# Order of TensorE in the first pairs of both MLP heads, and the place of the splits of squares

## The chip, the cores and the metric

The kernel runs on one core of a Trainium2 chip. The metric is the device time of one execution in microseconds (us); lower is better. The core has five engines with a queue each: TensorE (PE in the profile, its weight loads PEld) multiplies, VectorE (DVE), ScalarE (ACT) and GpSimd (POOL) work on elements, SyncE (SP) starts most transfers. An engine takes its own queue in order and waits on semaphores for the others.

## The reference

Two sequences of 512 tokens with 1024 features pass through a trunk of two layers. Cut to what matters:

```python
def sq_relu_mlp(h, w_up, w_down):
    a = jnp.maximum(h @ w_up, 0)
    return (a * a) @ w_down

def trunk(x, ...):
    for i in range(2):
        if i == 0:
            x = x + fourier_mix(rms_norm(x, fourier_norm), fourier_w_out)
        else:
            x = x + gqa_attention(rms_norm(x, attn_norm), ...)   # ends with o @ w_o
        x = x + sq_relu_mlp(rms_norm(x, mlp_norm[i]), w_up[i], w_down[i])
    return rms_norm(x, final_norm)
```

`rms_norm` divides a token's features by the root of their mean square and multiplies by a gain. Each MLP needs this norm over all 1024 features before its first product, and the output needs it once more.

## The kernel before, in words

Features lie on the partitions, tokens along the free dimension: `xt(q, fo)` is feature block `fo` (of 8) of sequence `q`, 128x512 in float32. Each float32 operand is split into a high half (a cast on ScalarE, line 86) and a low half (a subtraction on VectorE, line 87), and a product takes three matmuls per slice (`mm3`, lines 81 to 83, and `product`, line 962).

**The norm of transposed features.** `square` (line 167) squares a feature block on ScalarE; GpSimd adds the squares into `acc[q]` (line 171). With `alone=True` the last square is not added but kept in `apart[q]`. `Rows.split_all` splits `acc[q]` and, if there is one, `apart[q]` into halves. `Rows.root` multiplies them by a column of -1 on TensorE (line 206), which sums over the features; three activations follow on ScalarE (lines 207 to 209), and `Rows.rows` ends the row of inverse roots with two instructions on VectorE (lines 212 and 214). `Blocks.gain` (line 239) multiplies a feature block by its gain on ScalarE, `Blocks.norm` (line 254) by the row of inverse roots on VectorE.

**The MLP's two products** go by a Strassen-like scheme over blocks of both sequences. `Blocks.first` makes the operands `b11` (index 0 and 1) and `b21` (2 and 3) of sequence 0: norm, high half on ScalarE; `first_lo` makes the low half on VectorE (line 271). `second_sums` makes, for both sequences, norms, sums and differences (lines 311 to 323) and their halves, as a generator that the loop over pairs drives.

**The head of `first_product`.** Blocks of `w_up` come in pairs. Of the first `AHEAD` = 8 pairs, the loop computes the products with sequence 0 alone, while sequence 1's norm is being made: `Pair.first` multiplies by `b11` into a PSUM bank and copies it (ScalarE, line 995); `Pair.second` goes on in the same bank with `b21`, then come ReLU and square (lines 976 and 977). `split_row` splits a pair's weights (lines 86 and 87). Within the loop: `split_sums(1)` at p = 2, `root(1)` at p = 3, `spread(1)` (which is `Rows.rows`) at p = 4; second of pair 0 comes after second of pair 1. After the loop `rest` computes the remaining five products of each pair.

**W_o** ends attention and stands ahead of the second head. Blocks `m` = 0 to 3 are multiplied by operands `b11` and `b21`, then `t2`, `t3`, `t4`, and last `t1` and `b22` in the order of `turn()` (eight products, j = 0 to 7). In the t4 loop the add of line 1766 ends sequence 0's odd features, `square` and `gain` follow; after the loop comes `split_sums(0)`; in the last loop `root(0)` stands at j = 1 and `spread(0)` at j = 2, `first` and `first_lo` from j = 2 on.

**The tail** computes the last four blocks of the second MLP's down product. `project(0, fo)` and `project(1, fo)` run over eight feature blocks of sequence 0 and of half of sequence 1; between them `tokens(2)` and `tokens(3)` transpose two tiles of tokens, which `tile` computes with tokens on the partitions. `oa` and `ob` hold the output of the transposed part; `write` (line 1889) multiplies by the row of inverse roots and sends the output away.

**Who sets the order.** The Tile framework orders the instructions of each engine by its own plan from the dependencies. Within `tc.manual_schedule(engines={...})` the engines named take their instructions in the order written: all five in the tail, TensorE in the W_o part and in the second products, VectorE in part of `rest`. The head loop of `first_product` has no such block. `behind(x, y)` puts one instruction behind another in an engine's order without a semaphore.

Of the kernel before, what the change touches and what calls it, by code (L numbers as in the profile page):

```python
# [13 lines left out]
F32R = mybir.dt.float32r  # L14
BF16 = mybir.dt.bfloat16
AF = mybir.ActivationFunctionType
# [3 lines left out]
P = 128  # L20
# [24 lines left out]
def trunk_kernel(ctx, tc, x_in, xt_in, y_out, tables, rope, gfour, gcol, grow, gfin,  # L45
                 w_four, w_nyq, w_qkv, w_o, w_a22, w_up, w_row2, w_row4, w_sum2, w_sum4, w_down):
    nc = tc.nc
# [17 lines left out]
    def slot(shape, dt):  # L65
        return act.tile(shape, dt, tag="u4", name=nm("u"))
# [10 lines left out]
    def f32(ap):  # L77
        return ap.bitcast(F32)
# [6 lines left out]
    def split(dst_hi, dst_lo, src, eng=nc.vector):  # L85
        hi = nc.scalar.copy(dst_hi, src)  # L86
        return hi, eng.tensor_sub(dst_lo, src, f32(dst_hi))  # L87
# [64 lines left out]
    xs, acc, apart = {}, {}, {}  # L152
# [6 lines left out]
    def xt(q, fo):  # L159
        return xs[q, fo // 2][:, fo % 2]  # L160
# [23 lines left out]
    class Rows:  # L184
# [2 lines left out]
        def __init__(self, q, n=512):  # L187
            self.q, self.n, self.parts = q, n, []

        def split(self, x):  # L190
            h = slot([P, 2, self.n], F32R)
            made = split(h[:, 0], h[:, 1], x[:, : self.n])
            self.parts += [h[:, 0], h[:, 1]]
            return made

        def split_all(self):
            for x in [acc[self.q]] + ([apart.pop(self.q)] if self.q in apart else []):
                made = self.split(x)
            return made

        def root(self):
            n, o = self.n, ps()
# [25 lines left out]
    class Blocks:  # L228
# [7 lines left out]
        def gain(self, q, fo):  # L236
            if (q, fo // 2) not in self.f:
                self.f[q, fo // 2] = slot([P, 2, 512], F32)
            nc.scalar.activation(self.f[q, fo // 2][:, fo % 2], xt(q, fo), AF.Copy,
                                 scale=gc[:, self.g0 + fo : self.g0 + fo + 1])  # L240

        def split_sums(self, q):
            self.r[q] = Rows(q)
            return self.r[q].split_all()

        def root(self, q):
            self.r[q].root()
# [705 lines left out]
              for op in ROW + SUM} for l in range(2)]  # L953
    plain = [drm.tile([P, 2, 512], F32, name=f"plain_{f}") for f in range(2 * PLAIN)]

    def product(o, w, h, first=True):

        n = len(h)
        for k in range(n):
            sl = slice(k * P, (k + 1) * P)  # L960
            for i, (x, y) in enumerate(((0, 0), (0, 1), (1, 0))):
                nc.tensor.matmul(o, w[x][:, sl], h[k][y], start=first and k + i == 0,  # L962
                                 stop=k == n - 1 and i == 2, skip_group_check=not first)

    wo_added = []

    def first_product(l, blocks, rows, ahead):
# [120 lines left out]
        todo = blocks.second_sums()  # L1088
        pairs = [Pair(p) for p in range(NP)]
        for p in range(AHEAD):  # L1090
            if p == 4:
                blocks.spread(1)
            pair = pairs[p]
            if p < len(rows):
                pair.row = rows[p]
            else:
                pair.load()
                pair.split_row()
                if p == 3 and wo_added:
                    behind(pair.low, wo_added[0])  # L1100
            pair.first()
            if p == 2:
                blocks.split_sums(1)
            if p == 3:
                blocks.root(1)
            if p > 0:
                pair.second()
            if p == 1:
                pairs[0].second()
            if p > 3:  # L1110
                for _ in range(3):
# [653 lines left out]
    def add(x, o):  # L1765
        return nc.vector.tensor_add(x, o, x)
# [9 lines left out]
    with tc.manual_schedule(engines={ET.PE}):  # L1776
        o = {}
        for m, i in turn():
            if i == 0:
                o[m] = ps()  # L1780
            product(o[m], ahead[m][i], heads_out.operand(("b11", "b21")[i]), i == 0)
            if i:
                add(xs[0, m][:, 0], o[m])
                list(load_kept())
            else:
                nc.scalar.copy(e[m], o[m])
            if m + i > 1:
                next(todo)
        load_xs(1, park[1])
        o = {}  # L1790
        for k, name in enumerate(("t2", "t3", "t4")):
            h = heads_out.operand(name)
            for m in range(4):
                if k < 2:
                    o[m] = ps()
                product(o[m], ahead[4 + 2 * k + m // 2][m % 2], h, k < 2)
                if k == 0:
                    add(e[m], o[m])
                    square(0, 2 * m)
                    add(xs[0, m][:, 1], e[m])  # L1800
                elif k == 1:
                    add(xs[1, m][:, 1], o[m])
                    add(xs[1, m], e[m].unsqueeze(1).broadcast_to([P, 2, 512]))
                    blocks.gain(0, 2 * m)
                else:
                    add(xs[0, m][:, 1], o[m])
                    square(0, 2 * m + 1, alone=m == 3)
                    blocks.gain(0, 2 * m + 1)
                    put_away(0, m)
                if m % 2:  # L1810
                    list(load_kept())
                next(todo, None)
                if k == 2 and m < 2:
                    rows.append(halves(load_raw(w_up[1, 2 * m]), home=lent))
        o, lows = {}, []
        blocks.split_sums(0)
        for j, (m, i) in enumerate(turn()):
            if i == 0:
                o[m] = ps()
            product(o[m], ahead[10 + m][i], heads_out.operand(("t1", "b22")[i]), i == 0)  # L1820
            fo = 2 * m + 1 - i
            added = add(xt(1, fo), o[m])
            if 3 < j < 6:
                behind(lows[j - 4], added)
            square(1, fo, first=1)
            blocks.gain(1, fo)
            if i:
                put_away(1, m)
            if j == 1:
                blocks.root(0)  # L1830
            if j == 2:
                blocks.spread(0)
            if 1 < j < 6:
                normed = blocks.first(j - 2)
                if j == 5:
# [66 lines left out]
    with tc.manual_schedule(engines={ET.PE, ET.Activation, ET.DVE, ET.Pool, ET.SP}):  # L1902
        oa, ob, oc, oe = OutT(0, 4), OutT(1, 2), Out(2), Out(3)
        for fo in range(KC):
            project(0, fo, ws, [a[0] for a in ats])
            square(0, fo)
            oa.gain(fo)
        xtok = [tokens(2), tokens(3)]
        for fo in range(KC):
            project(1, fo, ws, [a[1] for a in ats], 256)  # L1910
            square(1, fo, 256, fo == KC - 1)
            ob.gain(fo)
            if fo == 1:
                oa.r.split_all()
            if fo == 2:
                oa.r.root()
            if fo == 3:
                oa.spread()
            if fo > 3:
                oa.write(fo - 4)  # L1920

        x, z = xtok
# [20 lines left out]
        def write(y, r, sl):  # L1943
            nc.scalar.activation(y[:, sl], y[:, sl], AF.Copy, scale=r)

        ob.r.split_all()
        o = [tile(2, 0, 512, 3, ob.r.root)]
        add(x, o[0], 0, 512)
        gain(x, y[0], 0)
# [191 lines left out]
```

## Time and profile before

| | |
|---|---|
| Median of three runs | 1674.67 us (1674.65 to 1674.84) |
| The profiled execution | 1674.12 us |
| Its span, first to last instruction | 1672.3 us |
| TensorE busy | 1656.0 us (99%) |
| VectorE busy | 1264.4 us (76%) |
| ScalarE busy | 884.9 us (53%) |
| GpSimd busy | 395.7 us (24%) |
| TensorE clock granted | 0.999 of full |

A row of the timeline has the start in us from the span's start, the length in us, engine and line, operation, output and inputs by the program's names, the count of instructions merged, and in brackets the idle time of the engine before it with what ended it. `PE ps L962` is a matmul of `product` into a PSUM bank. A page's row that groups instructions has their busy time and mean duration in ns. A row of windows has the stretch, its length, and for TensorE, its weight loads, VectorE, ScalarE and GpSimd the busy time with the count; then the granted clock, the share of the DMA engines and GB/s.

### The profile page before, as it was taken

How to read it: one execution, taken by the hardware profiler on the slowest of the kernel's cores; microseconds unless marked ns; L12 is line 12 of the kernel's file. 1: busy time of each engine (PE TensorE's matmuls, PEld its weight loads, DVE VectorE, ACT ScalarE, POOL GpSimd, SP SyncE). 2: the span in 40 equal slices, each digit the busy share in tenths (PEclk: the TensorE clock that was granted, in tenths of full speed). 3: DMA queues.
4: the chain of work that ended last, by engine and by line, in shares of the span. 5: the costliest groups of instructions: out<-in, count | busy, mean ns of one | idle time of the engine just before them, and what ended most of it. 6: DMA issues, size and time to landing. Idle time of an engine off the chain costs nothing.

```text
span 1672.3 us, 22127 instructions
## 1 busy us (share of the span) xinstructions
PE 1656.0 (99%) x7768; PEld 1379.8 (83%) x7768; DVE 1264.4 (76%) x1818; ACT 884.9 (53%) x1572; POOL 395.7 (24%) x365
## 2 busy tenths in 40 slices
PE   9999999999999999999999999999999999999997
PEld 8987888888888888888888888788888888888886
DVE  8889776557786879868788877777854487978865
ACT  7776444446343425448688855554544552433335
POOL 3331444221000001226444303004422220000002
PEclk9999999999999999999999999999999999999999
DMA  9843554459775757525401156335544696657522
GB/s 308 254 158 114 207 196 176 145 177 370 245 232 166 253 172 231 176 66 196 164 1 38 64 187 221 108 120 178 200 153 163 230 375 191 223 160 245 167 101 102
DMA packets 122193, 302.48 MB, mean 181 GB/s; under 512 B 12345, under 2 KB 13497, under 8 KB 122081
## 3 DMA queue, kind: packets, MB, share of 16 engines
q1 hardware_dynamic: 98720, 253.53, 43.4%
q0 software_dynamic: 8960, 21.05, 5.9%
q10 hardware_dynamic: 14400, 26.48, 4.2%
q8 instruction: 61, 1.00, 0.2%
q14 instruction: 52, 0.42, 0.1%
HBM read 217.59 MB, written 82.38 MB: 179 GB/s over the span
## 4 chain that ended last, share of the span: by engine, by line
PE 91%; DVE 6%; ACT 1%; issue 1%; DMA 0%; POOL 0%; DVEq 0%; SPq 0%; ACTq 0%; POOLq 0%
PE ps L962 71%; PE ps L83 6%; PE ps L81 6%; PE ps L82 6%; PE ps L1558 2%; DVE u L254 1%; DVE u L87 1%; DVE u L1889 0%; DVE u L271 0%; PE ps L1537 0%; DVE w L87 0%; ACT w L86 0%; DMA u<-x 0%; DVE t L214 0%; DVE u L312 0%
## 5 line engine op out<-in xcount | busy, mean ns | idle before, releaser
L962 PE MATMUL ps<-u,w 128*128 128x512 f32 x4944 | 1130.4, 389 | 3.4 <-DVE w L87 2.6
L962 PEld LDWEIGHTS ps<-u,w 128*128 128x128 f32 x4944 | 927.1, 188 | 199.1 <-DVE w L87 4.2
L86 ACT CAST w<-raw 128x1024 fp32r<-128x1024 f32 (+1 forms) x216 | 213.7, 994 | 306.6 <-PE ps L962 235.5
L87 DVE TENSOR_TENSOR w<-raw,w 128x1024 fp32r<-128x1024 f32 (+1 forms) x216 | 250.7, 1164 | 70.3 <-ACT w L86 67.1
L86 ACT CAST u<-u 128x1024 fp32r<-128x1024 f32 x144 | 145.0, 1050 | 86.9 <-PE ps L962 36.3
L87 DVE TENSOR_TENSOR u<-u,u 128x1024 fp32r<-128x1024 f32 x144 | 174.4, 1239 | 19.0 <-ACT u L86 18.0
L962 PE MATMUL ps<-u,u 128*128 128x512 f32 x600 | 143.2, 389 | 1.1 <-DVE t L1049 0.6
L1174 DVE TENSOR_TENSOR u<-ps,u 128x512 f32<-128x512 f32 x160 | 109.8, 688 | 40.1 <-PE ps L962 37.6
L1201 POOL DMA_DIRECT2D raw<-w_sum x32 | 27.7, 866 | 469.6 <-DMA raw<-w_sum 198.6
L1080 POOL TENSOR_TENSOR u<-u 128x512 f32<-128x512 f32 x28 | 37.8, 1350 | 425.5 <-ACT u L977 425.5
L962 PEld LDWEIGHTS ps<-u,u 128*128 128x128 f32 x600 | 112.5, 188 | 25.2 <-issue 1.0
L81 PE MATMUL ps<-u,u 128*128 128x512 f32 (+2 forms) x340 | 128.5, 380 | 0.0
L83 PE MATMUL ps<-u,u 128*128 128x512 f32 (+2 forms) x340 | 123.7, 365 | 0.0
L82 PE MATMUL ps<-u,u 128*128 128x512 f32 (+2 forms) x340 | 123.6, 365 | 0.0
L171 POOL TENSOR_TENSOR t<-t,t 128x512 f32<-128x512 f32 (+1 forms) x54 | 77.4, 1438 | 188.3 <-ACT t L167 187.3
L976 ACT ACTIVATE t<-t 128x512 f32<-128x512 f32 x64 | 40.5, 633 | 110.2 <-DVE t L1049 100.2
L87 DVE TENSOR_TENSOR u<-ps,u 128x512 fp32r<-128x512 f32 (+3 forms) x112 | 68.1, 635 | 6.2 <-ACT u L86 5.8
L83 PEld LDWEIGHTS ps<-u,u 128*128 128x128 f32 x340 | 64.2, 189 | 10.3 <-DVE u L87 0.3
L82 PEld LDWEIGHTS ps<-u,u 128*128 128x128 f32 x340 | 64.4, 189 | 8.7 <-DVE u L87 0.8
L81 PEld LDWEIGHTS ps<-u,u 128*128 128x128 f32 x340 | 64.4, 189 | 7.7
L1036 DVE TENSOR_TENSOR t<-ps,u 128x512 f32<-128x512 f32 x32 | 22.0, 689 | 61.0 <-PE ps L962 54.6
L1516 POOL TENSOR_TENSOR u<-t,t 128x256 f32<-128x256 f32 x40 | 51.0, 1286 | 62.4 <-DVE t L1514 46.4
(261 smaller groups left out, 2026.4 us busy)
## 6 DMA issues: line engine op xcount, KB each, us to landing
raw<-w_up SPq DMA_DIRECT2D x80, 512.0 KB, 4.5
u<-spill_t SPq DMA_DIRECT2D x60, 512.0 KB, 7.1
raw<-w_sum SPq DMA_DIRECT2D x56, 512.0 KB, 5.6
u<-spill_b SPq DMA_DIRECT2D x45, 512.0 KB, 6.4
spill_t<-u SPq DMA_DIRECT2D x84, 256.0 KB, 2.0
spill_b<-t ACTq DMA_DIRECT2D x60, 256.0 KB, 4.1
raw<-w_row SPq DMA_DIRECT2D x28, 512.0 KB, 4.7
park<-u SPq DMA_DIRECT2D x24, 512.0 KB, 4.1
```

The lines of the kernel that those rows point to most:

```text
L81: nc.tensor.matmul(out, lh, rh, start=first, stop=False)
L82: nc.tensor.matmul(out, lh, rl, start=False, stop=False)
L83: nc.tensor.matmul(out, ll, rh, start=False, stop=last)
L86: hi = nc.scalar.copy(dst_hi, src)
L87: return hi, eng.tensor_sub(dst_lo, src, f32(dst_hi))
L171: nc.gpsimd.tensor_add(acc[q][:, :n], acc[q][:, :n], s[:, :n])
L962: nc.tensor.matmul(o, w[x][:, sl], h[k][y], start=first and k + i == 0, stop=k == n - 1 and i == 2, skip_group_check=not first)
L976: nc.scalar.activation(t, src, AF.Relu)
L1080: eng.tensor_sub(t[:, 0], b12, b11)
L1174: return nc.vector.tensor_add(x, o, x)
L1516: nc.gpsimd.tensor_add(outs[(h0 + i) // 2].rearrange("p (h d) -> p h d", h=2), t1[:, i : i + 2], t2[:, i : i + 2])
L1558: nc.tensor.transpose(pt[:, t * P : (t + 1) * P], probs[t][:, sc * P : (sc + 1) * P], ident)
```

## The change

In both MLP heads TensorE takes pairs 0 to 2 in a written order: first 0; first 1, second 0, second 1; first 2, root of sequence 1, second 2. The splits of sequence 1's squares, its root and its spread stand one pair sooner in the program. In W_o sequence 0's splits move from behind the t4 loop to behind its last add, each with a place relative to the add, the last square and the gain; root 0 moves into the second product of the last loop (after two of its four slices), spread 0 one product ahead. In the tail sequence 0's high half moves between the two token transposes, its low half behind the first projection of sequence 1 and its root one projection ahead; two of the four writes of `oa` move behind the splits of `ob`. `Rows.split` is taken apart into `hi` and `lo`; the number of matmuls, splits, roots and writes stays.

```diff
 class Rows:
-        def split(self, x):
-            h = slot([P, 2, self.n], F32R)
-            made = split(h[:, 0], h[:, 1], x[:, : self.n])
+        def hi(self, x=None):
+            self.x, h = (acc[self.q] if x is None else x)[:, : self.n], slot([P, 2, self.n], F32R)
             self.parts += [h[:, 0], h[:, 1]]
-            return made
-        def split_all(self):
...
+            return nc.scalar.copy(h[:, 0], self.x)
+        def lo(self):
+            h, l = self.parts[-2:]
+            return nc.vector.tensor_sub(l, self.x, f32(h))
+        def split(self, x=None):
+            return self.hi(x), self.lo()
+        def split_alone(self):
+            return self.split(apart.pop(self.q))
...
-    def product(o, w, h, first=True):
+    def product(o, w, h, first=True, mid=None):
...
+            if mid and k == 1:
+                mid()
...
         for p in range(AHEAD):
-            if p == 4:
+            if p == 3:
                 blocks.spread(1)
...
-            pair.first()
-            if p == 2:
-                blocks.split_sums(1)
-            if p == 3:
-                blocks.root(1)
-            if p > 0:
-                pair.second()
-            if p == 1:
-                pairs[0].second()
+            with tc.manual_schedule(engines={ET.PE}) if p < 3 else nullcontext():
+                pair.first()
+                if p == 1:
+                    blocks.split_sums(1)
+                    pairs[0].second()
+                if p == 2:
+                    blocks.root(1)
+                if p > 0:
+                    pair.second()
...
                 else:
-                    add(xs[0, m][:, 1], o[m])
-                    square(0, 2 * m + 1, alone=m == 3)
-                    blocks.gain(0, 2 * m + 1)
+                    added = add(xs[0, m][:, 1], o[m])
+                    if m == 3:
+                        hi, lo = blocks.split_sums(0)
+                        behind(lo, added)
+                    squared = square(0, 2 * m + 1, alone=m == 3)
+                    if m == 3:
+                        behind(squared, hi)
+                        hi, lo = blocks.r[0].split_alone()
+                    gained = blocks.gain(0, 2 * m + 1)
+                    if m == 3:
+                        behind(gained, hi)
...
-        blocks.split_sums(0)
...
-            product(o[m], ahead[10 + m][i], heads_out.operand(("t1", "b22")[i]), i == 0)
+            product(o[m], ahead[10 + m][i], heads_out.operand(("t1", "b22")[i]), i == 0,
+                    (lambda: blocks.root(0)) if j == 1 else None)
...
             if j == 1:
-                blocks.root(0)
-            if j == 2:
                 blocks.spread(0)
...
-        xtok = [tokens(2), tokens(3)]
+        xtok = [tokens(2)]
+        oa.r.hi()
+        xtok.append(tokens(3))
         for fo in range(KC):
             project(1, fo, ws, [a[1] for a in ats], 256)
             square(1, fo, 256, fo == KC - 1)
             ob.gain(fo)
+            if fo == 0:
+                oa.r.lo()
             if fo == 1:
-                oa.r.split_all()
-            if fo == 2:
                 oa.r.root()
             if fo == 3:
                 oa.spread()
-            if fo > 3:
+            if 3 < fo < 6:
                 oa.write(fo - 4)
...
-        ob.r.split_all()
+        ob.r.split()
+        ob.r.split_alone()
+        for i in range(2, 4):
+            oa.write(i)
         o = [tile(2, 0, 512, 3, ob.r.root)]
```

More of the change, by code (lines that the diff above doesn't have):

```diff
@@ L188, in __init__ @@
             self.q, self.n, self.parts = q, n, []
-        def split(self, x):
-            h = slot([P, 2, self.n], F32R)
-            made = split(h[:, 0], h[:, 1], x[:, : self.n])
+        def hi(self, x=None):
+            self.x, h = (acc[self.q] if x is None else x)[:, : self.n], slot([P, 2, self.n], F32R)
             self.parts += [h[:, 0], h[:, 1]]
-            return made
-        def split_all(self):
-            for x in [acc[self.q]] + ([apart.pop(self.q)] if self.q in apart else []):
-                made = self.split(x)
-            return made
+            return nc.scalar.copy(h[:, 0], self.x)
[6 more added lines that the diff above has]
+            return self.split(apart.pop(self.q))
         def root(self):
@@ L238, in gain @@
                 self.f[q, fo // 2] = slot([P, 2, 512], F32)
-            nc.scalar.activation(self.f[q, fo // 2][:, fo % 2], xt(q, fo), AF.Copy,
-                                 scale=gc[:, self.g0 + fo : self.g0 + fo + 1])
+            return nc.scalar.activation(self.f[q, fo // 2][:, fo % 2], xt(q, fo), AF.Copy,
+                                        scale=gc[:, self.g0 + fo : self.g0 + fo + 1])
         def split_sums(self, q):
             self.r[q] = Rows(q)
-            return self.r[q].split_all()
+            return self.r[q].split()
         def root(self, q):
```

## The prediction

> **What bounds the kernel now.** I read the page first (busy time, chain), then TensorE's timeline alone, stretch by stretch, for its idle places, and last the other engines' timelines around each place.
>
> ```profile
> span 1672.3 us, 22127 instructions
> PE 91%; DVE 6%; ACT 1%; issue 1%; DMA 0%; POOL 0%; DVEq 0%; SPq 0%; ACTq 0%; POOLq 0%
> 1003.81 18.52 PE L962 MATMUL ps<-u,w 128*128 128x512 f32 x81
> ...
> 89.94 8.99 PE L962 MATMUL ps<-u,w 128*128 128x512 f32 x38
> 99.53 10.72 PE L962 MATMUL ps<-u,w 128*128 128x512 f32 x46 [0.60 <-DVE w L87]
> 128.57 11.63 PE L962 MATMUL ps<-u,w 128*128 128x512 f32 x50 [0.59 <-DVE w L87]
> 147.56 3.00 PE L962 MATMUL ps<-u,u 128*128 128x512 f32 x12 [0.56 <-DVE t L1049]
> 866.26 0.33 PE L1558 MATMUL ps<-ident,t 128*128 128x128 f32 x1 [0.23 <-POOL t L1552]
> 1037.64 2.57 PE L962 MATMUL ps<-u,w 128*128 128x512 f32 x10 [0.76 <-DVE u L1766]
> 1046.59 5.74 PE L962 MATMUL ps<-u,u 128*128 128x512 f32 x24 [0.50 <-ACT u L995]
> 1080.79 17.54 PE L962 MATMUL ps<-u,w 128*128 128x512 f32 x76 [1.42 <-DVE w L87]
> 1643.79 0.50 PE L206 MATMUL ps<-u,minus 128*128 128x512 f32 x1 [0.50 <-ACT u L86]
> 1644.52 0.51 PE L206 MATMUL ps<-u,minus 128*128 128x512 f32 x1 [0.23 <-DVE u L87]
> 1655.99 1.25 PE L206 MATMUL ps<-u,minus 128*128 128x256 f32 x4 [1.03 <-ACT u L86]
> ```
>
> TensorE is on 91% of the chain, so time is won only where TensorE waits. The number of matmuls doesn't change. In the timeline of TensorE (start, length, count; in brackets the idle time before and what ended it) the first row gives the pace: 81 matmuls start within 18.52 - 0.39 us, 0.227 us each, while one row of 389 ns overlaps the next. So a bracket understates a wait by 0.39 - 0.23 = 0.16 us.
>
> Between 89 and 148 us (head of the first MLP) and between 1004 and 1081 us (W_o and head of the second) these are all of TensorE's waits. Their true prices: from 89.94 us 38 matmuls should end their turn at 98.55, and the next starts at 99.53: **0.98**. Then 0.59 + 0.16 = **0.75** and 0.56 + 0.16 = **0.72**; in the second head 0.76 + 0.16 = **0.92**, 0.50 + 0.16 = **0.66**, 1.42 + 0.16 = **1.58**. Heads: 2.45 and 3.16 us. From 148 to 1004 us I found one other wait, 0.23 us in attention, and none from 1081 to 1643. What the heads win therefore travels to the end undiluted.
>
> **The change part by part.**
>
> *First head: pairs 0 to 2 in a written order.* Products have 12 matmuls (four operand slices by three), 2.72 us.
>
> ```profile
> 91.75 1.65 DVE L271 TENSOR_TENSOR u<-u,u 128x1024 fp32r<-128x1024 f32 x1
> 97.45 2.02 DVE L87 TENSOR_TENSOR w<-raw,w 128x1024 fp32r<-128x1024 f32 x1 [0.28 <-ACT w L86]
> 102.36 0.63 ACT L86 CAST u<-t 128x512 fp32r<-128x512 f32 x1 [0.62 <-POOL t L171]
> 110.09 0.63 PE L206 MATMUL ps<-u,minus 128*128 128x512 f32 x2
> 117.08 2.36 DVE L254 TENSOR_TENSOR u<-u,t 128x1024 f32<-128x1024 f32 x2
> 104.00:117.00 13.00, 13.00 (x59) 10.73 (x58) 6.15 (x7) 10.35 (x16) 0.00 (x0) 1.00 0.48 157
> 117.00:130.00 13.00, 12.40 (x55) 9.97 (x54) 13.00 (x13) 5.82 (x9) 0.00 (x0) 1.00 0.22 73
> L995 ACT COPY u<-ps 128x512 f32<-128x512 f32 x32 | 18.4, 584 | 8.3 <-PE ps L962 8.3
> L86 ACT CAST u<-u 128x1024 fp32r<-128x1024 f32 x144 | 145.0, 1050 | 86.9 <-PE ps L962 36.3
> ```
>
> The 38 matmuls are three products and two more: TensorE ran the first products of pairs 0, 1 and 2 and began pair 3, whose weight split (L87) ends at 99.47. The written order is first 0, first 1, second 0, second 1, first 2, root, second 2, so pair 3 comes some 9 us later, when its split is long done. Second 0 would start at 89.94 + 24 x 0.227 = 95.4; its operand's last low half (L271) ends at 93.40. The 0.98 goes.
>
> The root of sequence 1 is then due after five products, at 103.6, against 110.09. GpSimd's sums end just before ScalarE's cast at 102.36, which ends at 102.99; the low half (0.69 us) can be there by 103.7, or at 104.2 if it stays behind VectorE's present work: up to 0.4 us of wait, and it lies beside the next one. That next one is new: second 2 stands right behind first 2 and two root matmuls. It writes the bank that first 2's copy reads: 0.39 for the last matmul, 0.58 for the copy and some 0.1 to hand over are 1.07 us, of which 3 x 0.227 are covered: **0.40 us** of wait (none if the root itself waits; 1.45 if a 1.05-us cast stands ahead of the copy in ScalarE's queue).
>
> The two rows of windows (TensorE, its weight loads, VectorE, ScalarE, GpSimd, each busy time and count) carry the rest: VectorE has 6.9 us idle in 104 to 117 and none in 117 to 130. The norm of sequence 1 (L254) starts at 117.08 and everything behind it, the splits for which TensorE waits at 128.57 and 147.56 included, stands in that full queue. A root 6.5 us earlier lets norm and sums start in the idle time; 0.75 and 0.72 ask for less than a quarter of it. Both go. Net for the first head: 2.45 - 0.40 = **2.05 us**.
>
> *W_o and second head.*
>
> ```profile
> 1017.76 0.69 DVE L87 TENSOR_TENSOR u<-t,u 128x512 fp32r<-128x512 f32 x1 [2.85 <-ACT u L86]
> 1018.37 0.68 DVE L1766 TENSOR_TENSOR u<-ps,u 128x512 f32<-128x512 f32 x1
> 1020.88 0.69 DVE L87 TENSOR_TENSOR u<-t,u 128x512 fp32r<-128x512 f32 x1 [0.53 <-ACT u L86]
> 1022.17 1.09 PE L206 MATMUL ps<-u,minus 128*128 128x512 f32 x4
> 1024.25 0.67 ACT L207 ACTIVATE u<-ps,eps 128x512 f32<-128x512 f32 x1
> 1026.03 0.69 DVE L1766 TENSOR_TENSOR u<-ps,u 128x512 f32<-128x512 f32 x1 [2.97 <-PE ps L962]
> 1043.70 4.10 DVE L271 TENSOR_TENSOR u<-u,u 128x1024 fp32r<-128x1024 f32 x2
> 1045.97 1.05 ACT L995 COPY u<-ps 128x512 f32<-128x512 f32 x2
> 1060.39 0.63 PE L206 MATMUL ps<-u,minus 128*128 128x512 f32 x2
> 1026.00:1047.00 21.00, 19.74 (x86) 15.71 (x86) 20.97 (x18) 16.15 (x23) 10.28 (x6) 1.00 0.33 126
> 1047.00:1064.00 17.00, 17.00 (x75) 13.67 (x74) 7.67 (x9) 7.99 (x14) 0.00 (x0) 1.00 0.38 131
> ```
>
> Now the first low half (L87, 1017.76) stands ahead of the add (1018.37) that ends sequence 0's last features: the add waits for a cast although its matmuls ended by 1017. Putting low behind add, and the last square behind the high half, turns this round. The add ends about 1017.6, the last square 1018.3, its low half 1019.7 instead of 1021.6. The root, put after 6 of the second t1/b22 product's 12 matmuls, comes at 1022.17 - 1.36 = 1020.8 with its operands there. ScalarE's logarithm, now at 1024.25 behind that product's square and gain, can start at 1022.0: about 2.2 us earlier, and VectorE's idle 2.97 us before 1026.03 takes in the chain. From 1026 to 1047 VectorE is busy 20.97 of 21 us, so the lead of some 2 us passes down its queue: the add that holds TensorE at 1037.64 needs 0.92 of it. At 1046.59 TensorE waits because ScalarE's copies start only at 1045.97, behind work that waits for VectorE; 2 us sooner they are clear of it. The low halves of b21 (L271, ending 1047.80) move to about 1045.8; TensorE, 0.92 us earlier, needs the last at its eighth matmul of second 0, at 1046.6. Both waits go.
>
> The root of sequence 1 comes after second 1 and first 2, at about 1053.2 against 1060.39; VectorE is idle 9.3 of the 17 us from 1047 to 1064, so the norm leads by some 7 us and the 1.58 at 1080.79 goes. The copy behind first 2 costs 0.40 again. Net: 3.16 - 0.40 = **2.76 us**.
>
> *Tail, all engines in written order.*
>
> ```profile
> 1643.14 0.60 ACT L86 CAST u<-t 128x512 fp32r<-128x512 f32 x1
> 1649.89 1.21 DVE L1889 TENSOR_TENSOR u<-u,t 128x1024 f32<-128x1024 f32 x1
> 1654.72 1.42 DVE L1889 TENSOR_TENSOR u<-u,t 128x1024 f32<-128x1024 f32 x1
> 1656.06 0.75 DVE L87 TENSOR_TENSOR u<-t,u 128x256 fp32r<-128x256 f32 x2
> 1656.73 0.68 DVE L1937 TENSOR_TENSOR u<-ps,u 128x512 f32<-128x512 f32 x1
> 1658.70 0.42 DVE L212 SCALAR_TENSOR_TENSOR u<-ps,u 128x256 f32<-128x256 f32 x1 [0.56 <-ACT u L209]
> ```
>
> The first root's wait is 0.50 + 0.16 us, and 0.50 more between its two matmuls (0.73 apart instead of 0.23): 1.2 us. So it was due at 1643.13, and one product earlier (12 matmuls of 256 columns, 0.12 us each) at 1641.7. Sequence 0's cast moves from 1643.14 to between the two token transposes' copies, about 1640.2, its low half behind the first add, ending near 1641.5: that wait goes. The later root waits 1.03 + 0.16 and then again between its four matmuls, 1.8 us in all, because ScalarE's last square waits for an add that stands behind a write (L1889). It was due at 1654.8, now 1.2 earlier, 1653.6; the last sequence-1 product ends a 2.72-us tile before that, at 1650.9. With two writes out of the way its add ends about 1651.4, square and gain 1652.2, the two casts 1653.0, the low halves (0.75 us for two in the row) 1653.4: in time. So TensorE leaves the tail about 3 us earlier. But it doesn't set the end there: VectorE does, working without a break from 1656.06 except 0.56 us. The two postponed writes (1.21 us each without GpSimd beside them, 1.13 apart) now stand between the low halves and the add of L1937: 1653.33 + 2 x 1.13 = 1655.6 against 1656.73, a lead of 1.1; the 0.56 wait for ScalarE goes as well, since the root's three activations end at about 1655.6. I take **1.7 us**, between 0.5 (a GpSimd add still beside the writes) and 3.0 (TensorE's own gain). The writes' DMAs on SP follow them; nothing waits for these but the end, where later ones stand behind them.
>
> Here a rule bears: by the Trainium skill, "SBUF — State Buffer", section "Who interferes with whom", a VectorE instruction with two SBUF inputs and a GpSimd instruction that reads SBUF lock each other out for a whole instruction. The trace agrees in direction (a write takes 1.21 us alone and 1.42 beside an add), and by that rule the postponed writes would cost less than they did.
>
> *Sum*: 2.05 + 2.76 + 1.7 = 6.5 us. The profiled execution took 1674.12 us (span 1672.3), 0.55 below the median of the runs, so 1667.6 against its own time and **1668.2 us** against the median, 0.39% less.
>
> **The rivals.** (a) *VectorE's and ScalarE's queues, which are not written out in the heads, keep their present order*, and the early roots help no one: the waits at 128.57, 147.56 and 1080.79 stay, 3.05 us: 1671.2. Against it: those queues have the idle time shown. (b) *The earlier norms collide with GpSimd's adds.* L271 takes 2.05 us a piece at 1043.70 beside them and 1.65 at 91.75. If the lead of 2 us is eaten, 0.92 and 0.66 stay: 1669.7. The skill's page named above is the rule behind it. Against it: as many adds as now, beside the same kind of work. (c) *The tail's end doesn't move*, since the writes take back what the splits give: 1669.9. (d) *TensorE's waits only move on*, to weights or operands that come late further on, and only the tail remains: 1673.0. (e) *Slower: the pinned root blocks TensorE.* In a written order nothing can pass a root that waits for its low half. If the splits keep the places that let the root come at 110.09 and 1060.39, TensorE stands 6.5 and 7.2 us; for the two waits of 0.40 that makes 6.5 + 0.8 - 13.7 = -6.4, so 1681. It decides from 6.5 us of added waits on. Against it: the cast at 102.36 already comes within 1.3 us of the new due time.
>
> **How the numbers follow.** Forecast 0.56 (with its own range of 1666.9 to 1669.3), (a) 0.13, (b) 0.08, (c) 0.09, (d) 0.08, (e) 0.06. A measurement of this kernel tells 0.2%, 3.35 us, from no change: the line lies at 1671.3. The forecast, (b), (c) and half of (a) are faster: 0.80; (d) and half of (a) the same: 0.14; (e) slower: 0.06. The range ends below at 1666.4, with 3.0 in the tail and part of the two 0.40 us unpaid, and above at 1671.4, which takes in (a), (b) and (c) and leaves out (d) and (e).
>
> **What would show it.** After: no wait before pair 3's weights; the root of sequence 1 near 103.6 and near 1052; VectorE's idle time in the heads moved behind the second sums; no TensorE wait on L1766; a wait of about 0.4 us on a copy (L995) behind each sequence-1 root; in the tail roots without a wait and VectorE unbroken to the end. Wrong would be: a root waiting over 1 us for a low half, a new wait of TensorE on weight splits in pairs 3 to 7, or an end that stays while TensorE finishes earlier.

## The result and the profile after

The changed kernel takes 1671.16 us (median of 13 runs, 1670.01 to 1672.34) against 1674.52 us on the same chip (13 runs, 1674.05 to 1675.94): ratio 0.9979, 95% interval [0.9971, 0.9988], so 3.4 us less and faster. The forecast was 1668.2 us, 6.5 less; a little over half of it came. The profiled execution took 1670.05 us, 4.07 less than that of before (1674.12). Two executions far off the rest, one of experiment 8 (2796.3 us, granted clock 0.556) and one of the kernel before (7155.22 us), are left out of the medians further down.

TensorE's timeline after, as before: all its waits of more than 0.2 us from 89 us to the end, and four of the roots.

```profile
90.05 8.54 PE L966 MATMUL ps<-u,w 128*128 128x512 f32 x36
100.94 5.74 PE L966 MATMUL ps<-u,w 128*128 128x512 f32 x24 [2.35 <-ACT u L1001]
106.52 0.63 PE L210 MATMUL ps<-u,minus 128*128 128x512 f32 x2
106.99 41.59 PE L966 MATMUL ps<-u,w 128*128 128x512 f32 x180
866.62 0.33 PE L1564 MATMUL ps<-ident,t 128*128 128x128 f32 x1 [0.23 <-POOL t L1558]
1021.27 1.09 PE L210 MATMUL ps<-u,minus 128*128 128x512 f32 x4
1045.78 5.73 PE L966 MATMUL ps<-u,u 128*128 128x512 f32 x24 [0.29 <-ACT u L1001]
1054.07 0.63 PE L210 MATMUL ps<-u,minus 128*128 128x512 f32 x2
1651.21 0.63 PE L210 MATMUL ps<-u,minus 128*128 128x256 f32 x4
```

(L966 is the old L962, L1001 the copy of L995, L210 the root of L206.) The waits at 99.53, 128.57, 147.56, 1037.64 and 1080.79 us and all three of the tail are gone. One has come: at 100.94 TensorE stands for the copy of a pair's first product, after 36 matmuls, which is three first products. By the working that gave 0.98 us (36 x 0.227 from 90.05 are over at 98.22) its price is 2.72 us, more than the 2.45 us that went in that head.

The same instruction in both traces gives the account. The transpose behind the short wait near 866 us starts at 866.62 instead of 866.26: 0.36 later. Then three VectorE rows of after: an add of W_o, the first half-width add of the tail, and the last multiplication.

```profile
1014.67 0.69 DVE L1772 TENSOR_TENSOR u<-ps,u 128x512 f32<-128x512 f32 x1 [2.03 <-PE ps L966]
1638.14 0.42 DVE L950 TENSOR_TENSOR u<-ps,u 128x256 f32<-128x256 f32 x1 [2.49 <-PE ps L83]
1663.76 0.75 DVE L2004 TENSOR_SCALAR u<-u,s 128x512 f32<-128x512 f32 x2
```

Before, they were:

```profile
1014.21 0.69 DVE L1766 TENSOR_TENSOR u<-ps,u 128x512 f32<-128x512 f32 x1 [2.03 <-PE ps L962]
1640.45 0.42 DVE L946 TENSOR_TENSOR u<-ps,u 128x256 f32<-128x256 f32 x1 [2.49 <-PE ps L83]
1667.86 0.75 DVE L1987 TENSOR_SCALAR u<-u,s 128x512 f32<-128x512 f32 x2
```

So after stands +0.46, -2.31 and -4.10 us against before. The first head's products begin 0.11 late (90.05 against 89.94, from the start of the program), so the first head itself **lost 0.25** up to 866 us, where 2.05 of gain had been forecast; W_o and the second head won **2.77** (forecast 2.76); the tail won **1.79** (forecast 1.7). Another 0.10 is lost between 866 and 1014 us, where nothing was changed. This account is of two single executions, 4.1 us apart; the medians are 3.4 apart, and no row here says where the other 0.7 us lie.

Why TensorE waits at 100.94 is seen on ScalarE, after:

```profile
98.58 0.61 ACT L167 ACTIVATE t<-u 128x512 f32<-128x512 f32 x1
99.10 1.32 ACT L243 ACTIVATE u<-u,gc 128x512 f32<-128x512 f32 x2
100.33 1.04 ACT L1001 COPY u<-ps 128x512 f32<-128x512 f32 x2
102.45 0.62 ACT L193 CAST u<-t 128x512 fp32r<-128x512 f32 x1 [1.07 <-POOL t L171]
102.97 0.58 ACT L1001 COPY u<-ps 128x512 f32<-128x512 f32 x1
```

The copy of pair 0 stands in ScalarE's queue behind the last squares and gains (L167, L243) of the stage ahead, which is written in a fixed order for all engines. It starts at 100.33 and can't start sooner, though its product was over at 92.8 (12 x 0.227 from 90.05). Second of pair 0 goes on in the bank that this copy reads, so it can't start before about 100.9. Before, the copies stood in the same place, and TensorE had more first products to do meanwhile:

```profile
100.22 1.53 ACT L995 COPY u<-ps 128x512 f32<-128x512 f32 x3
```

And why three first products, where the forecast had two: each of the three written blocks has its own order, but nothing orders one block against the next. In the trace TensorE takes first 0, first 1, first 2, then second 0 (with the wait), second 1, the root, second 2. First 2, from the third block, slipped ahead of the second block's second 0; its copy is the last row above, at 102.97. Why the plan put it there is not shown.

### The profile page after: what moved, and what is told of

Same layout as the page of the kernel before. It is cut to its first block, busy times and chain, and to the rows that moved or that the text cites. A ratio compares the mean times of both kernels' runs of the same rounds, so it can differ in the third digit from the quotient of the medians.

```text
span 1668.2 us, 22126 instructions
## 1 busy us (share of the span) xinstructions
PE 1653.6 (99%) x7768; PEld 1379.2 (83%) x7768; DVE 1267.9 (76%) x1818; ACT 884.1 (53%) x1572; POOL 394.0 (24%) x365
## 4 chain that ended last, share of the span: by engine, by line
PE 94%; DVE 4%; ACT 1%; issue 1%; DMA 0%; POOL 0%; DVEq 0%; ACTq 0%; POOLq 0%
PE ps L966 74%; PE ps L83 6%; PE ps L81 6%; PE ps L82 6%; PE ps L1564 2%; DVE u L258 0%; DVE u L275 0%; PE ps L1543 0%; DVE u L1901 0%; DVE u L432 0%; DVE u L1772 0%; DMA g<-gfour 0%; ACT t L167 0%; ACT u L243 0%; PE ps L529 0%
## 5 line engine op out<-in xcount | busy, mean ns | idle before, releaser
L966 PE MATMUL ps<-u,w 128*128 128x512 f32 x4944 | 1130.2, 389 | 2.4 <-ACT u L1001 2.4
L966 PEld LDWEIGHTS ps<-u,w 128*128 128x128 f32 x4944 | 927.2, 188 | 197.6 <-ACT u L1001 5.0
L966 PE MATMUL ps<-u,u 128*128 128x512 f32 x600 | 143.1, 389 | 0.3 <-ACT u L1001 0.3
L966 PEld LDWEIGHTS ps<-u,u 128*128 128x128 f32 x600 | 112.6, 188 | 24.0 <-ACT u L1001 0.7
L86 ACT CAST u<-ps 128x512 fp32r<-128x512 f32 (+3 forms) x112 | 59.2, 555 | 7.5 <-PE ps L1564 5.8
```

## The experiments

Times are medians; "before" ran on the same chip beside each. Theory A throughout: the first head's gain is lost to the copies' place in ScalarE's queue, and each other part wins what the forecast said.

**1. One written block instead of three**, in both heads, so that TensorE's order is the one the forecast had read:

```diff
+        one = ExitStack()
         for p in range(AHEAD):
+            if p == 0:
+                one.enter_context(tc.manual_schedule(engines={ET.PE}))
             if p == 3:
+                one.close()
                 blocks.spread(1)
...
-            with tc.manual_schedule(engines={ET.PE}) if p < 3 else nullcontext():
+            with nullcontext():
```

> Changed kernel with one written TensorE block over pairs 0 to 2 in both heads (first 0, first 1, second 0, second 1, first 2, root, second 2), where the change has three separate blocks between which first 2 slips ahead of second 0. Theory A (in the first head second 0 waits for ScalarE's copy of pair 0, which comes at 100.9 us behind squares and gains whatever TensorE does): TensorE now arrives 12 matmuls earlier, at 95.5, still goes on only at 100.9, and the copy's wait grows from 2.35 to about 5.1 us; the kernel is about 2.7 us slower than the changed one, near 1673.9. Rival B (the order of TensorE was the loss; in the order as predicted the wait is at most 0.4 us): about 2 us faster than the changed kernel, near 1669.

1674.96 us against 1673.95, ratio 1.0007 [0.9998, 1.0016]. TensorE's timeline:

```profile
100.52 10.84 PE L966 MATMUL ps<-u,w 128*128 128x512 f32 x36 [5.25 <-ACT u L1001]
```

The wait is A's: one first product less to do, 2.9 us more to stand. The time is 1.1 us longer than A's 1673.9, and B falls. The windows (stretch, length, then TensorE, weight loads, VectorE, ScalarE and GpSimd busy, the granted clock, DMA share, GB/s) say where:

```profile
101.00:104.00 3.00, 3.00 (x8) 2.32 (x8) 2.77 (x3) 0.62 (x1) 0.94 (x1) 0.50 0.01 3
104.00:107.00 3.00, 3.00 (x11) 2.35 (x11) 0.00 (x0) 1.07 (x2) 0.00 (x0) 0.73 0.00 0
```

Behind the wait TensorE ran at half its clock: 8 matmuls in 3 us where after has 13, and 10.84 us for 36 where 36 took 8.54 in after at full clock.

**2. The first products and copies of pairs 0 and 1 of the first head moved into the stage ahead**, ahead of its last squares and gains on ScalarE:

```diff
+        def begin_first():
+            t, o = slot([P, 2, 512], F32), ps()
+            product(o, rows[len(firsts)][0], blocks.operand("b11"))
+            nc.scalar.copy(t[:, 0], o)
+            firsts.append((t, o))
...          # stage ahead, after the odd features' fourth block
+                begin_first()
+                begin_first()
...          # Pair.first
+                if l == 0 and self.p < 2:
+                    self.t, self.o = firsts[self.p]
+                    return
```

> Changed kernel with the first products of pairs 0 and 1 of the first head and their copies written into the front part, the copies around the weight cast of pair 3, ahead of the last two squares and three gains in ScalarE's queue. Theory A (the copy's place in ScalarE's queue costs 2.35 + 0.16 us): the wait on the copy near 98 to 101 us goes, about 2.4 us faster than the changed kernel, near 1668.7, 5.8 us less than before. Rival B (something else is late there, the sums of squares or a weight split, and the wait only changes its name): within 0.5 us of the changed kernel.

1667.93 us (5 runs) against 1673.95, ratio 0.9966 [0.9954, 0.9979]: 6.0 us less, as A expects. What is left of the first head's wait:

```profile
104.79 0.98 PE L210 MATMUL ps<-u,minus 128*128 128x512 f32 x2
106.98 40.66 PE L760 MATMUL ps<-u,w 128*128 128x512 f32 x176 [0.29 <-ACT u L1012]
```

So once the copies are out of the way, the first head pays most of what had been forecast: this version is 1.7 us below version 3 (next), which differs from it in the first head's part alone, and the forecast for that part was 2.05. The copy's wait of 0.29 + 0.16 us behind the root is the one that had been priced at 0.40; the two root matmuls take 0.98 us here instead of 0.63, since the second waits.

**3. The changed kernel with the old loop in the first head.**

```diff
-            if p == 3:
+            if p == (4 if l == 0 else 3):
                 blocks.spread(1)
...
+            if l == 0:
+                pair.first()
+                if p == 2:
+                    blocks.split_sums(1)
+                if p == 3:
+                    blocks.root(1)
+                if p > 0:
+                    pair.second()
+                if p == 1:
+                    pairs[0].second()
+            else:
                 with tc.manual_schedule(engines={ET.PE}) if p < 3 else nullcontext():
```

> Changed kernel with the old loop over pairs in the first head alone (W_o, second head and tail stay changed). Theory A (the first head gives nothing: 2.51 us of new wait on the copy against 0.98 + 0.75 + 0.72 won): within 0.5 us of the changed kernel or up to 1 us faster, 1670 to 1671.2, about 4.5 us below the kernel before by the profile. Rival B (the early root pays in the first head as forecast): about 2 us slower than the changed kernel. Rival C (the new wait of 2.35 us costs more than its length in some executions, since TensorE's clock drops around it: the changed kernel's runs spread from 1670.0 to 1672.3 at mean clocks of 0.997 to 0.999): the runs of this kernel spread less and their median is 1 us or more below the changed kernel's.

1669.65 us against 1673.95, ratio 0.9975 [0.9965, 0.9985]: 4.3 less, 0.9 more of a gain than with the first head's part. The two intervals overlap, so the 0.9 is not clear of noise, but Rival B, which had 2 us *less* gain, falls. Rival C stays open: seven of the eight runs lie between 1669.34 and 1670.40 us, the eighth at 1671.9.

**4. The new loop in the first head alone**: the same branch taken for `l == 1`, and W_o and tail as before.

```diff
-            if p == 3:
+            if p == (4 if l == 1 else 3):
...
+            if l == 1:      # the old loop, as in 3
```

> Kernel before with the new loop over pairs in the first head alone. Theory A: no gain, between 0 and 1 us slower than the kernel before (0.25 us by the stage's wait in the profile), with the wait on the copy of 2.3 us. Rival B: 2 us faster. Rival C (clock): median 1 us or more slower than before, with a wider spread.

1675.7 us against 1673.95, ratio 1.001 [1.0001, 1.0018]: 1.75 *more*. The old waits of that head are gone, the new one is there:

```profile
100.11 7.33 PE L966 MATMUL ps<-u,w 128*128 128x512 f32 x24 [2.36 <-ACT u L1001]
```

and the windows behind it:

```profile
101.00:104.00 3.00, 3.00 (x10) 2.33 (x9) 2.41 (x3) 1.10 (x2) 0.57 (x1) 0.56 0.01 3
104.00:107.00 3.00, 3.00 (x13) 2.46 (x12) 0.84 (x1) 2.06 (x3) 0.00 (x0) 0.87 0.00 0
```

In this execution the wait itself loses 0.25 us as in after, and the clock 1.59 more: 24 matmuls took 7.33 us instead of the 5.74 in after, whose wait of the same length (2.35) was followed by full clock. The time is outside A's 0 to 1 us; it is Rival C's, whose wider spread came too (3.4 us from lowest to highest, against 1.7 for before).

**5. The wait filled with 16 matmuls on spare data**, to see whether the granted clock is what spreads and lifts the changed kernel's times (its profiled execution is 1.1 below its own median):

```diff
                 pair.first()
+                if l == 0 and p == 2:
+                    idle(ps(), 16)
```

> Changed kernel with 16 filler matmuls (128x256, about 0.12 us each, 1.9 us in all) written behind first 2 in the first head, where TensorE waits 2.35 us for ScalarE's copy. They add no work to the path if the copy's hour holds; their product is not used. Theory A (the wait has two prices: its own 2.5 us, and in most executions a drop of TensorE's granted clock behind it, as in the kernel with the first head's loop alone, whose clock was 0.56 in 101 to 104 us): the copy's hour stays at 100.9, the rest of the wait is below 0.6 us, mean clocks are 0.999, the runs spread less than 1 us apart from the spread that the kernel before has, and the median is about 1 us below the changed kernel's. Rival B (the clock has nothing to do with the wait; the changed kernel's spread of 1670.0 to 1672.3 comes from elsewhere): same median and same spread as the changed kernel.

1671.26 us (1669.92 to 1672.27) against 1674.28, ratio 0.9982 [0.9973, 0.9991]. The wait shrank to 0.43 us at 101.24, and neither the median nor the spread got better. So that the clock lifts the changed kernel's median is not shown. The mean clocks speak for a part of it: four of the changed kernel's 13 runs have 0.997 (1671.59 to 1672.34 us), none of the 11 here. But the profiled execution here took 1671.84 us with a granted clock of 1.00 from 98 to 107 us; it has a wait that after doesn't have, behind VectorE, which stood for weights from a DMA (here first, then the same row in after):

```profile
1208.73 3.01 PE L966 MATMUL ps<-u,w 128*128 128x512 f32 x12 [0.78 <-DVE t L1046]
1199.86 1.70 DVE L1017 TENSOR_TENSOR raw<-raw,raw 128x512 f32<-128x512 f32 x1 [2.70 <-DMA raw<-w_up]
1198.26 0.69 DVE L1017 TENSOR_TENSOR raw<-raw,raw 128x512 f32<-128x512 f32 x1 [1.58 <-DMA raw<-w_up]
```

So executions differ in more than the clock; how the 2.3 us divide stays open.

**6. As 2, and in the second head the two copies put ahead of the last square and the last gain on ScalarE:**

```diff
-                pair.first()
+                copied = pair.first()
+                if l and p < 2:
+                    behind(last_acts[2 + p], copied)
```

> The kernel with the first head's copies early, and in the second head too the copies of pairs 0 and 1 put ahead of the last square and the last gain in ScalarE's order. Theory A: the wait of 0.28 + 0.16 us at 1045 us goes; 0.4 us below the kernel with the first head's copies early, near 1667.5. Rival B (the square behind the copy delays GpSimd's sum and with it the root of sequence 1): the wait moves to the root, no gain.

1667.52 us (1667.34 to 1668.2, 5 runs) against 1674.28, ratio 0.9962 [0.9948, 0.9975]: 6.8 us less, A's time. From 89 us on, TensorE's only waits of more than 0.2 us are these of 0.27 and 0.23 us, so B's wait at the root didn't come:

```profile
105.74 40.68 PE L760 MATMUL ps<-u,w 128*128 128x512 f32 x176 [0.27 <-ACT u L1012]
864.48 0.33 PE L1577 MATMUL ps<-ident,t 128*128 128x128 f32 x1 [0.23 <-POOL t L1571]
```

The head's products begin here at 89.71 us (89.94 before) and the transpose at 864.48 (866.26 before): by the account used above the first head wins 1.55 us.

**7 to 9. The tail alone, W_o alone, the second head's loop alone**, each with the rest as before. From the changed kernel, what is taken back:

```diff
# 7: pair loops and W_o taken back; 8: pair loops and tail; 9: first head, W_o and tail
+            if True:        # the old loop of 3 in both heads (7, 8), with l == 0 in 9
...
-                        hi, lo = blocks.split_sums(0)       # W_o (7, 9)
+        blocks.split_sums(0)                                # after the t4 loop
...
-        oa.r.hi()                                           # tail (8, 9)
+            if fo == 1:
+                oa.r.split()
```

> Kernel before with the new tail alone. Theory A (VectorE's queue sets the end, not TensorE): 1.8 us faster than before, TensorE about 3 us ahead of its old place at the last root. Rival B (TensorE sets the end): 3 us faster. Rival C (the postponed writes take back the gain): 0 to 0.5 us.

1672.39 us against 1674.28, ratio 0.999 [0.9981, 0.9999]: 1.9 less, A's time; C falls. The last root, at 1655.99 before, and spread there over 1.25 us:

```profile
1653.49 0.63 PE L210 MATMUL ps<-u,minus 128*128 128x256 f32 x4
```

Its end is 3.1 us sooner than before's, and the kernel's only 1.9: TensorE doesn't set the end, and B falls.

> Kernel before with the new W_o part alone (early splits and root of sequence 0; pairs and tail as before). Theory A (W_o's early root gives VectorE 2 us of lead): the waits at 1037.64 and part of that at 1046.59 go, 0.9 to 1.6 us faster, while the 1.58 us at 1080.79 stays, since the second head's root of sequence 1 is not earlier. Rival B (the lead alone also carries the wait at 1080.79 away): 3 us faster.

1672.90 us against 1674.28, ratio 0.9993 [0.9984, 1.0002]: 1.4 less, not told from nothing by the interval. In its trace:

```profile
1044.69 5.73 PE L966 MATMUL ps<-u,u 128*128 128x512 f32 x24 [0.29 <-ACT u L1001]
1078.90 17.56 PE L966 MATMUL ps<-u,w 128*128 128x512 f32 x76 [1.42 <-DVE w L87]
```

The add's wait (0.76 before) is gone, the weights' wait stays, so B falls.

> Only the second head's loop is changed (splits of squares of sequence 1 behind the first product of pair 1, root behind that of pair 2, spread at pair 3); first head, W_o and tail are those of the kernel before. Theory A (each part wins the waits that stand behind it, and the second head's loop wins what the full change won less W_o and tail): TensorE's wait of 1.42 us (1.58 true) at 1080.8 is gone, those of 0.76 at 1037.6 and about 0.5 at 1046.6 stay; the root of sequence 1 starts some 6 us sooner than 1060.39. The time falls by 1.1 to 1.6 us, to about 1673 against 1674.3. Rival B (the loop helps only once W_o's part has let sequence 0's chain lead, because VectorE is full from 1026 to 1047): the wait at 1080.8 stays at 0.7 us or more, and the time falls by under 0.7 us.

1672.65 us against 1674.17, ratio 0.999 [0.9981, 0.9999]: 1.5 less. Here it is the other way round:

```profile
1037.12 3.02 PE L966 MATMUL ps<-u,w 128*128 128x512 f32 x12 [0.77 <-DVE u L1783]
1046.08 5.74 PE L966 MATMUL ps<-u,u 128*128 128x512 f32 x24 [0.50 <-ACT u L1001]
1054.38 0.63 PE L210 MATMUL ps<-u,minus 128*128 128x512 f32 x2
```

and no wait near 1080 (its rival, that the loop needs W_o's lead, falls). The four parts add up: +1.75 - 1.4 - 1.9 - 1.5 = -3.05, against -3.4 for all. Each has an interval of about 1.5 us to either side, so the waits in the traces show the parts better than the times do.

**10. Two of the tail's writes put back into its loop**, in the version of 6:

```diff
-            if 3 < fo < 6:
+            if fo > 3:
                 oa.write(fo - 4)
...
-        for i in range(2, 4):
-            oa.write(i)
```

> The version with early copies in both heads (1667.52 us, 6.8 below the kernel before), with two of the tail's four multiplications of sequence 0's output (the writes) put back into the loop over sequence 1's features, so that only the splits and the root of the tail stay earlier. Theory A (it is the early splits that win in the tail; the writes cost VectorE the same wherever they stand, and they stand now where it otherwise waits): the last add of the loop is late by about 1 us, the second root comes about 0.9 us later than in that version, and the end moves by 0.1 to 0.4 us at most; time 1667.5 to 1668.0. Rival B (putting the two writes off is what wins): the end comes 1 us or more later, TensorE waits over 1 us for the second root's splits, and the time is 1668.6 to 1669.3.

1667.59 us against 1674.17, ratio 0.9958 [0.9945, 0.997], 6.6 us less, where 6 is 6.8 less. The first half-width add of the tail and the last multiplication here, then in 6:

```profile
1636.48 0.42 DVE L969 TENSOR_TENSOR u<-ps,u 128x256 f32<-128x256 f32 x1 [2.49 <-PE ps L83]
1649.63 1.19 PE L210 MATMUL ps<-u,minus 128*128 128x256 f32 x4
1661.43 0.75 DVE L2017 TENSOR_SCALAR u<-u,s 128x512 f32<-128x512 f32 x2
```

```profile
1635.46 0.42 DVE L969 TENSOR_TENSOR u<-ps,u 128x256 f32<-128x256 f32 x1 [2.49 <-PE ps L83]
1648.53 0.63 PE L210 MATMUL ps<-u,minus 128*128 128x256 f32 x4
1661.08 0.75 DVE L2019 TENSOR_SCALAR u<-u,s 128x512 f32<-128x512 f32 x2
```

In the traces the tail is 24.95 us here and 25.62 in 6: 0.67 *shorter*, where A expected 0.1 to 0.4 longer and B a microsecond longer. A's time came, but by its account of the end both missed. The second root comes 13.15 us after that add instead of 13.07, and its four matmuls take 1.19 instead of 0.63 because they wait between them; but VectorE has no two writes (2.35 us) between the low halves and the add behind them. So by these two traces the early splits win the tail, and putting the writes off gives part of it back; the medians don't tell the two versions apart.

**11. The changed kernel without any written order in the pair loops:**

```diff
-            with tc.manual_schedule(engines={ET.PE}) if p < 3 else nullcontext():
+            with nullcontext():
```

> The changed kernel without the written order of TensorE in the first three pairs of both heads: the program's text keeps the splits, roots and spreads where the change put them, and nothing else is undone. Theory A (the three separate written blocks pin nothing that the planner wouldn't choose; what acts is the earlier place of splits, root and spread in the program): TensorE's order, its wait of about 2.35 us behind the third first product of the first head and the time are those of the changed kernel, 1670 to 1672.4, median 1671.2. Rival B (the written blocks keep other matmuls out of the wait): the wait in the first head falls below 1.5 us, and the time below 1670.5.

1670.88 us (1669.12 to 1672.14) against 1674.17, ratio 0.9978 [0.9969, 0.9986]: the changed kernel's time. So is its wait:

```profile
100.69 5.75 PE L966 MATMUL ps<-u,w 128*128 128x512 f32 x24 [2.33 <-ACT u L1001]
```

The three written blocks decide nothing here. What is left to act is where splits, root, spread and second of pair 0 stand in the program.

## Why the prediction was right or wrong

The direction was right and the time lies in the range, near its upper end (1671.16 of 1671.4), but outside the forecast's own 1666.9 to 1669.3. By the two traces the size was wrong by the first head alone; the 0.7 us between traces and medians stay open.

- **First head, 2.05 forecast, -0.25 measured: the failed step.** It is the sentence that let second 0 start at 95.4 once "its operand's last low half (L271) ends at 93.40". Second 0 also needs its bank's copy, and the trace of before had that copy at 100.22 (L995, three of them). The forecast priced a copy only behind first 2. As it read the order the wait would have been 5.3 us, as experiment 1 shows; 2.35 came only because three blocks aren't one order. Experiments 2 and 6 take the copies out of the way and come near the forecast's time (6.0 and 6.8 us less, 6.5 forecast; 6 also takes away a copy's wait in the second head). The head itself then wins 1.55 to 1.7 of the 2.05.
- Its other parts held. The waits at 128.57 and 147.56 are gone: the norm (L258) starts at 113.54 instead of 117.08, in what was VectorE's idle time. The root was 2.9 us later than forecast (106.52 against 103.6), since the wait stands ahead of it.

```profile
113.54 4.62 DVE L258 TENSOR_TENSOR u<-u,t 128x1024 f32<-128x1024 f32 x4
```

- **The new copy wait of 0.40 behind each sequence-1 root didn't come.** In the first head first 2 had slipped ahead, so its copy (102.97) was long over when second 2 began behind the root at 106.99. In the second head two matmuls of pair 3's first product stand between the root and second 2.
- **W_o and second head, 2.76 forecast, 2.77 measured**, partly by luck: the wait at 1046.59, priced 0.66, was to go and left 0.29 + 0.16 = 0.45, which replaces the 0.40 that didn't come. The steps held: the add starts at 1017.39, its two low halves at 1018.21 and 1019.44, the first logarithm at 1022.40 (forecast 1022.0), the root of sequence 1 at 1054.07 (forecast 1053.2). Experiments 8 and 9 price the two parts at 1.4 and 1.5 us.

```profile
1017.39 0.69 DVE L1772 TENSOR_TENSOR u<-ps,u 128x512 f32<-128x512 f32 x1 [2.03 <-PE ps L966]
1018.21 0.69 DVE L197 TENSOR_TENSOR u<-t,u 128x512 fp32r<-128x512 f32 x1
1019.44 0.69 DVE L197 TENSOR_TENSOR u<-t,u 128x512 fp32r<-128x512 f32 x1 [0.54 <-ACT u L193]
1022.40 0.69 ACT L211 ACTIVATE u<-ps,eps 128x512 f32<-128x512 f32 x1 [0.32 <-PE ps L210]
```

- **Tail, 1.7 forecast, 1.79 measured**, 1.9 alone. VectorE sets the end: unbroken behind the low halves, with the two writes ahead of the add of L1951.

```profile
1650.33 0.76 DVE L197 TENSOR_TENSOR u<-t,u 128x256 fp32r<-128x256 f32 x2 [1.24 <-ACT u L193]
1651.01 2.35 DVE L1901 TENSOR_TENSOR u<-u,t 128x1024 f32<-128x1024 f32 x2
1653.28 0.68 DVE L1951 TENSOR_TENSOR u<-ps,u 128x512 f32<-128x512 f32 x1
```

The add leads by 1.14 us beyond the tail's start (forecast 1.1), and the wait of 0.56 us for ScalarE is gone too. The forecast counted on two writes being out of the way; experiment 10 keeps them in the loop, and its tail is 0.67 us shorter still. The two writes take 2.35 us together here and 1.42 or 1.43 each beside GpSimd's adds, in the direction that the Trainium skill gives ("SBUF — State Buffer", section "Who interferes with whom"). The forecast read 1.21 us as a write alone; in its trace an add ran into that write (from 1650.57), and it was the add that took longer, 1.13 us instead of 0.73.
- **Of the rivals**, (a) named 1671.2 us, the time that came, but by chance: the three waits that it kept are gone. (b) falls with the 0.92 that went, though 0.45 of its 0.66 stayed; its two durations of L271 didn't show what it took from them, since GpSimd's adds ran beside the row at 91.75 as well. (c) falls by the tail's 1.79, though experiment 10 shows the writes taking back 0.67. (d), waits that only move on, is what happened in the first head, at another place than any named: not to weights or operands but to a copy. (e), a pinned TensorE that stands, was the right kind of danger with the wrong cause: the sequence-1 roots never waited; second 0 did, and not because of the pinning.

## What to carry to other kernels

When a matmul is moved sooner, list everything that frees its bank, not only its operands, and look in the trace at when that instruction runs today and what stands ahead of it in its engine's queue. An order written in several blocks is several orders; read the order that came from the trace before any price is put on it. A wait that TensorE fills with other ready products costs nothing until a change takes those products away.

## What was not expected of the hardware

A wait of TensorE can cost more than its length. In experiment 4 a wait of 2.36 us was followed by a granted clock of 0.56 and 0.87 over the next two stretches of 3 us, 1.59 us more for 24 matmuls; in experiment 1 one of 5.25 us by 0.50 and 0.73, 2.30 us more for 36 (10.84 against 8.54). In the profile of after a wait of 2.35 us left it at 1.00, as did one of 2.33 us in experiment 11:

```profile
101.00:104.00 3.00, 3.00 (x13) 2.49 (x14) 2.93 (x4) 1.48 (x4) 1.41 (x1) 1.00 0.00 0
```

The Trainium skill ("TensorE: Matmul & The Clock Gate", section "What's actually happening") puts the drop at an idle window of about 3.4 us and says that the window runs free of the program. A free window fits a loss that comes in one run and not in another; the length doesn't fit experiment 4, whose 2.36 us were enough. What decides it was not tried.
